# Block products of the gate and up tiles written two at a time, in the matmul order of the plain products

## The chip, the cores and the metric

The kernel runs on one core of a Trainium2 chip. The metric is the device time of one launch in microseconds (us), median of several runs. A core has five engines that each work through a queue of their own in order: PE (TensorE, matrix products), DVE (VectorE), ACT (ScalarE), POOL (GpSimd) and SP (SyncE, which here only issues DMAs). PE loads a 128 x 128 weight tile and then streams columns of a moving operand through it; results accumulate in PSUM, whose banks DVE and ACT read. Everything else lies in SBUF.

## The reference

One step of a hybrid streaming encoder layer, in fp32, on 512 prompt frames and 64 frames of a running stream (576 columns together, the same weights for both):

```python
def swiglu_ffn(x, w_gate_up, w_down):
    gate, up = jnp.split(x @ w_gate_up, 2, axis=-1)
    return (jax.nn.silu(gate) * up) @ w_down
...
    x = x + 0.5 * swiglu_ffn(rms_norm(x, ffn1_norm), ffn1_w_gate_up, ffn1_w_down)
    h = rms_norm(x, mix_norm)
    p = h @ w_in
...
    x = x + merged @ w_out
    x = x + 0.5 * swiglu_ffn(rms_norm(x, ffn2_norm), ffn2_w_gate_up, ffn2_w_down)
```

The model width is 1024, the FFN's inner width 2816. Between the two FFNs stands the mixer: a projection to seven blocks of 1024, two depthwise convolutions with gates, and three more 1024 x 1024 products. A final RMSNorm follows.

## The kernel before

**Layout.** Features lie on the 128 partitions, frames in the columns, so an activation is a list of 128 x 576 tiles. A moving operand is one half of such a tile: columns 0 to 287 (the first half) or 288 to 575 (the second half); H is 288. The two halves' results go to the two PSUM banks of one tile made by `psum2()`; there are four such tiles.

**Precision.** Each fp32 value is split in a high part (type fp32r) and a low part, the rest. A product takes three matmuls: weight high by activation high, weight high by activation low, weight low by activation high. `SIX` (L56) is the order in which a plain product does its six, for each 128 rows of the contraction: high-high and high-low on the first half, the same on the second, then low-high on the first and on the second half.

**FFN.** The 22 inner tiles of 128 go in four groups (`GROUPS`, L42: 5, 5, 6 and 6 tiles). A group makes its hidden tiles (gate, up, SiLU, product) and then multiplies them by its rows of `w_down` into 8 output tiles; the first two of these are interleaved by `both`. The first `PLAIN` tiles (3 in the first FFN, 1 in the second) use plain products. The rest, 19 and 21, use `pair` (L735): a scheme that replaces the eight half-size block products of gate and up by seven, on sums and differences of weight blocks and activations. Each of the seven block products contracts 512 features (KU = 4 tiles), has 288 columns and so 4 x 3 = 12 matmuls. Which half of a tile each of the seven streams is set by `Forms.operands`:

```python
return first[:KU], t2, t1, t3, first[KU:], second[KU:], t4
```

`first` and `second` are the halves of the normed input, t1 and t3 first halves and t2 and t4 second halves of the summed tiles. So products 1, 5 and 6 (counted from 0) stream second halves and the other four first halves.

**Order of work in a pair.** For each block product n: fetch its weight unit (`ws.get`), take a bank (`bank()`, the two banks of a PSUM tile in turn), issue its 12 matmuls one after another, then issue the DVE and ACT steps of product n-1 (`steps`: copies, sums and differences, and in `gate` the SiLU). What remains of a pair (`up`, `hidden`, `parts`) waits in `rest` and is issued one step after each product of the next pair.

**Weights.** `Stream` holds the weight units in the order of their use. SP loads raw weights (six buffers). `add` forms sums of blocks on DVE. `begin` casts the high part on ACT; for three of the seven units of a pair (products 0, 4 and 6) it also writes the negated high part on ACT and lets a POOL DMA add the raw weights to it, which gives the low part. For the other four a DVE subtraction (`end`) gives it. `get(n)` runs this ahead: casts are issued up to six units past n. High and low parts take slots in turn in two pools of eight buffers, so eight units fit; a cast waits until PE has used the unit that had the slot.

Of the kernel before, what the change touches and what calls it, by code (L numbers as in the profile page):

```python
# [10 lines left out]
AF = mybir.ActivationFunctionType  # L11
ALU = mybir.AluOpType
# [5 lines left out]
FT = DFF // P  # L18
SEQ = 512
DSEQ = 64  # L20
KU = KT // 2
T = SEQ + DSEQ
H = T // 2
# [27 lines left out]
PLAIN = {"f1": 3, "f2": 1}  # L51
# [4 lines left out]
SIX = ((0, 0), (1, 0), (0, 1), (1, 1), (2, 0), (2, 1))  # L56
# [47 lines left out]
def tile_encoder_step(  # L104
# [41 lines left out]
    def ttile(dt=F32):  # L146
        return tmp.tile([P, T], dt, tag="tmp", name=nm("tmp"))

    def psum2():
        return mmps.tile([P, 2, 512], F32, tag="mm", name=nm("mm"))  # L150

    spare = []

    def bank():

        if not spare:
            t = psum2()
            spare.extend((t[:, 0, :], t[:, 1, :]))
        return spare.pop(0)

    def halves(ap):
        return ap.rearrange("p (s n) -> p s n", s=2)
# [1 line left out]
    def half(ap, s):  # L164
        return ap[:, s * H : (s + 1) * H]
# [27 lines left out]
    class Stream:  # L193
# [108 lines left out]
    ws = Stream(6)  # L302
    plan = {}
# [60 lines left out]
    for k in FIRST_KS:  # L364
        for name in FIRST:
            r = ws.raw(ffn1_gu, row, k, gu_col(*name[1:]))
# [49 lines left out]
    behind = []  # L416
# [189 lines left out]
    xg = []  # L606
# [83 lines left out]
    def ffn(f, xg, sums, finish, forms, R=None, todo=()):  # L690
        todo = list(todo)

        rest = []


        def plain(i, hs):
# [35 lines left out]
                for step, p in todo.pop(0):  # L732
                    step(p)

        def pair(i, hs, last):  # L735
            qu, uu, t, cu = (ttile() for _ in range(4))
            q1, u2, u3, u4 = half(qu, 0), half(qu, 1), half(uu, 0), half(uu, 1)
            q = []

            def q7():  # L740
                dve.tensor_tensor(u3, q[3], u2, op=ALU.add)
                dve.tensor_tensor(half(cu, 1), u3, q[2], op=ALU.subtract)

            def gate():
                dve.tensor_tensor(half(t, 1), q[5], u4, op=ALU.add)
                dve.tensor_tensor(t, t, R, op=ALU.mult)
                sca.activation(t, t, AF.Silu)

            steps = (
                lambda: sca.copy(q1, q[0]),  # L750
                lambda: dve.tensor_tensor(u2, q[1], q1, op=ALU.subtract),
                lambda: dve.tensor_tensor(u4, q[2], u2, op=ALU.subtract),
                q7,
                lambda: dve.tensor_tensor(half(t, 0), q[4], q1, op=ALU.add),
                gate,
            )
            for n, xs in enumerate(bs):
                w = ws.get(plan[f, "s", i][n])
                q.append(bank()[:, :H])
                for k in range(KU):  # L760
                    (whi, wlo), (xh, xl) = w, xs[k]
                    for m, (l, r) in enumerate(((whi, xh), (whi, xl), (wlo, xh))):
                        pe.matmul(
                            q[n], l[:, k, :], r, start=k == m == 0, stop=k == KU - 1 and m == 2
                        )
                if n > 0:
                    steps[n - 1]()
                if rest:
                    rest.pop(0)()

            hs.append(None)
            at = len(hs) - 1

            def up():
                if last:
                    dve.tensor_tensor(t, t, R, op=ALU.mult)
                dve.tensor_tensor(half(cu, 0), q[6], u3, op=ALU.add)

            def hidden():
                dve.tensor_tensor(cu, cu, t, op=ALU.mult)  # L780
                hs[at] = high(cu)

            def parts():
                hs[at] = hs[at], low(cu, hs[at])

            rest.extend((up, hidden, parts))

        for g, grp in enumerate(GROUPS):
            hs = []
            for i in grp:  # L790
                if i < PLAIN[f]:
                    plain(i, hs)
                    continue
                if i == PLAIN[f]:
                    bs = forms.operands(xg)
                pair(i, hs, grp[-1] == FT - 1)
            while rest:
                rest.pop(0)()
            spare.clear()
            if grp[-1] < FT - 1:  # L800
                for j, ps in enumerate(both([(f, "d", g, j) for j in range(2)], hs)):
                    update(j, ps, R)
                for j in range(2, KT):
                    update(j, product((f, "d", g, j), hs), R)
            else:
                finish(g, hs)
# [390 lines left out]
```

## Time and profile before

| What | Value |
|---|---|
| median of three runs | 1302.98 us (1302.82 to 1303.01) |
| the profiled execution's own time | 1303.07 us |
| its span, first to last instruction | 1301.3 us |
| granted TensorE clock, mean | 0.998 |
| DMA, mean over the span | 168 GB/s |

Engines' busy times count a matmul from its start to its modelled end; matmuls overlap, so a busy PE does not tell at what pace they follow each other. That is read from starts on the timeline, where one row merges neighbouring instructions of one group: the start in us, the time from the start of the first to the end of the last, engine, line, operation, tiles (written<-read, buffer numbers left out), shape, and how many. The names of weight tiles are `u`, `g` and `act`, by the pool that the unit lies in; they change from unit to unit, so that a row of matmuls ends where the unit changes. The line is always L80, that of a helper which keeps the program's order. In brackets stands the engine's idle time before the row and what ended it.

### The profile page before, as it was taken

Reading aid. Unit: us, or ns where it says so; the run is one execution under the profiler, and the core shown is the slowest. Engines: PE = TensorE matmul, PEld = TensorE weight load, DVE = VectorE, ACT = ScalarE, POOL = GpSimd, SP = SyncE. Lnnn points to the kernel's source line nnn. Section 1 sums busy time; section 2 is a strip of 40 time slices with the busy share of each in tenths; the row PEclk is TensorE's granted clock in tenths of the full one; section 3 lists DMA queues with packets and bytes.
Section 4 is the critical chain, followed back from the end, with each engine's and each line's share of the span. In section 5 each row is a group of like instructions: output and inputs, shape, how many; then the busy total and the mean of one; then the engine's idle time right before and its main releaser. Section 6 shows DMA issues by size and latency. Waiting matters only on the chain.

```text
span 1301.3 us, 25714 instructions
## 1 busy us (share of the span) xinstructions
PE 1286.3 (99%) x9746; PEld 1282.5 (99%) x9746; DVE 892.0 (69%) x1460; ACT 778.5 (60%) x1374; POOL 400.5 (31%) x502
## 2 busy tenths in 40 slices
PE   9999999999999999999999999999999999999997
PEld 8999999999999999999999999999999999999996
DVE  6758758748945899888895260336967848847955
ACT  8755655645677655555554684457665655654664
POOL 4242332332242544322221322222142141241233
PEclk9999999999999999999999999999999999999999
DMA  9797787886798797877775978776687796796784
GB/s 245 141 189 160 148 185 157 165 192 147 152 195 182 167 216 173 175 166 170 172 168 125 199 158 178 154 166 142 138 169 165 162 192 149 163 206 136 161 178 107
DMA packets 290108, 218.40 MB, mean 168 GB/s; under 512 B 15680, under 2 KB 251200, under 8 KB 289984
## 3 DMA queue, kind: packets, MB, share of 16 engines
q0 software_dynamic: 60768, 100.30, 46.4%
q1 hardware_dynamic: 227488, 115.62, 31.4%
q8 instruction: 77, 1.26, 0.4%
q10 hardware_dynamic: 1728, 0.84, 0.2%
q14 instruction: 47, 0.39, 0.1%
HBM read 113.81 MB, written 2.62 MB: 89 GB/s over the span
## 4 chain that ended last, share of the span: by engine, by line
PE 90%; issue 4%; DMA 2%; ACT 1%; POOL 1%; DVE 1%; DVEq 0%; POOLq 0%; ACTq 0%; SPq 0%
PE mm L80 90%; DMA g<-raw 1%; DMA raw<-in_ffn_w_gate_up_dram 1%; POOL act L80 1%; DVE tmp L80 0%; ACT u L80 0%; DMA gains<-in_params_dram 0%; POOL g L80 0%; ACT tmp L80 0%; ACT g L80 0%; DVE acc L80 0%; ACT act L80 0%; DVE x L80 0%; DVE g L80 0%; POOL tmp L80 0%
## 5 line engine op out<-in xcount | busy, mean ns | idle before, releaser
L80 PE MATMUL mm<-act,u 128*128 128x288 f32 x4686 | 660.9, 294 | 0.7 <-DVE u L80 0.5
L80 PEld LDWEIGHTS mm<-act,u 128*128 128x128 f32 x4686 | 630.9, 188 | 1.2 <-DVE u L80 0.7
L80 PE MATMUL mm<-act,g 128*128 128x288 f32 x2766 | 398.6, 294 | 2.1 <-DMA g<-raw 2.0
L80 PEld LDWEIGHTS mm<-act,g 128*128 128x128 f32 x2766 | 376.5, 188 | 2.9 <-DMA g<-raw 2.8
L80 POOL DMA_DIRECT2D u<-raw x204 | 176.3, 864 | 550.4 <-ACT u L80 492.2
L80 PE MATMUL mm<-act,act 128*128 128x288 f32 (+2 forms) x2244 | 307.6, 293 | 1.4 <-DVE act L80 1.4
L80 PEld LDWEIGHTS mm<-act,act 128*128 128x128 f32 x2244 | 297.8, 188 | 2.4 <-DVE act L80 2.1
L80 POOL DMA_DIRECT2D g<-raw x124 | 108.6, 876 | 247.2 <-ACT g L80 188.2
L80 ACT CAST u<-raw 128x512 fp32r<-128x512 f32 (+2 forms) x204 | 117.1, 574 | 108.6 <-PE mm L80 76.5
L80 DVE SCALAR_TENSOR_TENSOR w<-g,prm,w 128x606 f32<-128x606 f32 x232 | 179.3, 844 | 1.4 <-ACT w L80 1.4
L80 DVE TENSOR_TENSOR tmp<-mm,tmp 128x288 f32<-128x288 f32 (+1 forms) x244 | 109.7, 458 | 72.9 <-PE mm L80 53.5
L80 ACT ACTIVATE u<-u 128x512 fp32r<-128x512 f32 (+2 forms) x204 | 121.1, 594 | 6.5
L80 POOL DMA_DIRECT2D act<-raw x90 | 78.9, 876 | 50.6 <-ACT act L80 49.5
L80 DVE SCALAR_TENSOR_TENSOR tmp<-mm,r 128x576 f32<-128x576 f32 x48 | 36.3, 757 | 78.0 <-PE mm L80 77.8
L80 ACT CAST g<-raw 128x512 fp32r<-128x512 f32 (+2 forms) x124 | 67.7, 546 | 35.3 <-DMA raw<-in_ffn_w_down_dram 14.7
L80 ACT CAST act<-tmp 128x576 fp32r<-128x576 f32 x84 | 56.2, 674 | 52.4 <-DVE tmp L80 51.6
L80 ACT CAST g<-w 128x512 fp32r<-128x512 f32 x80 | 49.6, 619 | 63.0 <-DVE w L80 56.6
L80 ACT CAST u<-w 128x512 fp32r<-128x512 f32 x80 | 49.5, 619 | 61.9 <-DVE w L80 55.7
L80 DVE TENSOR_TENSOR act<-tmp,act 128x576 fp32r<-128x576 f32 x80 | 59.3, 754 | 21.3 <-ACT act L80 19.8
L80 ACT ACTIVATE g<-g 128x512 fp32r<-128x512 f32 (+2 forms) x124 | 70.4, 568 | 3.9
L80 ACT CAST act<-raw 128x512 fp32r<-128x512 f32 (+2 forms) x99 | 57.6, 583 | 16.1 <-PE mm L80 11.0
L80 DVE TENSOR_TENSOR w<-raw,raw 128x512 f32<-128x512 f32 x80 | 54.8, 685 | 11.0 <-DMA raw<-in_ffn_w_gate_up_dram 11.0
(88 smaller groups left out, 814.1 us busy)
## 6 DMA issues: line engine op xcount, KB each, us to landing
raw<-in_ffn_w_gate_up_dram SPq DMA_DIRECT2D x173, 256.0 KB, 3.4
u<-raw POOLq DMA_DIRECT2D x145, 256.0 KB, 4.0
raw<-in_w_in_dram SPq DMA_DIRECT2D x112, 256.0 KB, 3.4
act<-raw POOLq DMA_DIRECT2D x80, 256.0 KB, 4.8
raw<-in_ffn_w_down_dram SPq DMA_DIRECT2D x96, 192.0 KB, 3.5
g<-raw POOLq DMA_DIRECT2D x65, 256.0 KB, 3.8
g<-raw POOLq DMA_DIRECT2D x43, 192.0 KB, 4.5
u<-raw POOLq DMA_DIRECT2D x43, 192.0 KB, 4.5
```

The source lines that it names most:

```text
L80: return self.tc.keep_in_program_order(fn(*args, **kwargs))
```

## The change

The seven block products of all pairs of a group are put in one list, `jobs`, and written two at a time. A PSUM tile's two banks hold the two products of a two, and the matmuls of both go in the order of `SIX`, with "product" in the place of "half": per 128 rows of the contraction, high-high and high-low of the one, the same of the other, then low-high of each. Seven is odd, so twos run on over the border of pairs: 0 with 1, 2 with 3, 4 with 5, 6 with 0 of the next pair, 1 with 2, 3 with 4, 5 with 6. In the groups with an odd number of products the last one goes alone. Both weight units are fetched before the first matmul of a two. The steps behind a product (`behind`) are issued after the next two's matmuls, those of both products of the two together; each is followed by one step out of `rest`. `bank` and `spare` are gone. The steps themselves are the same.

```diff
-            for n, xs in enumerate(bs):
-                w = ws.get(plan[f, "s", i][n])
-                q.append(bank()[:, :H])
...
+        def pairs(ps):
+
+            jobs = [(p, n) for p in ps for n in range(7)]
+            before = []
+            for c in range(0, len(jobs), 2):
+                two = jobs[c : c + 2]
+                out = psum2()
+                ops = []
+                for s, (p, n) in enumerate(two):
+                    p.q.append(out[:, s, :H])
+                    ops.append((ws.get(plan[f, "s", p.i][n]), bs[n]))
                 for k in range(KU):
-                    (whi, wlo), (xh, xl) = w, xs[k]
-                    for m, (l, r) in enumerate(((whi, xh), (whi, xl), (wlo, xh))):
-                        pe.matmul(
-                            q[n], l[:, k, :], r, start=k == m == 0, stop=k == KU - 1 and m == 2
-                        )
-                if n > 0:
-                    steps[n - 1]()
-                if rest:
-                    rest.pop(0)()
...
+                    for m, s in SIX:
+                        if s < len(two):
+                            (whi, wlo), (xh, xl) = ops[s][0], ops[s][1][k]
+                            l, r = ((whi, xh), (whi, xl), (wlo, xh))[m]
+                            pe.matmul(
+                                out[:, s, :H], l[:, k, :], r,
+                                start=k == m == 0, stop=k == KU - 1 and m == 2,
+                            )
+                for p, n in before:
+                    p.behind(n)
+                    if rest:
+                        rest.pop(0)()
+                before = two
+            for p, n in before:
+                p.behind(n)
```

On PE, at the start of the first FFN's first pair, before: the first rows of product 0. A row is: line, operation, PSUM tile written, moving operand (`act`, high and low part in turn), weights (`g_96` and `g_97` are the high and low part of unit 0, `u_98` and `u_99` of unit 1), shape.

```order
L80 MATMUL mm_157_742<-act_3_110,g_96_464 128x288
L80 MATMUL mm_157_742<-act_4_111,g_96_464 128x288
L80 MATMUL mm_157_742<-act_3_110,g_97_465 128x288
L80 MATMUL mm_157_742<-act_14_134,g_96_464 128x288
L80 MATMUL mm_157_742<-act_15_135,g_96_464 128x288
L80 MATMUL mm_157_742<-act_14_134,g_97_465 128x288
```

The same place on PE, of the change:

```order
L80 MATMUL mm_147_724<-act_3_110,g_96_464 128x288
L80 MATMUL mm_147_724<-act_4_111,g_96_464 128x288
L80 MATMUL mm_147_724<-act_77_278,u_98_493 128x288
L80 MATMUL mm_147_724<-act_102_524,u_98_493 128x288
L80 MATMUL mm_147_724<-act_3_110,g_97_465 128x288
L80 MATMUL mm_147_724<-act_77_278,u_99_494 128x288
```

Unit 1's high part has moved from the 13th to the 3rd matmul and its low part from the 15th to the 6th; unit 0's low part from the 3rd to the 5th.

On ACT, in the second group of the first FFN, at the end of a pair, before. The ACTIVATE on `tmp` is the pair's SiLU; a CAST into `u` or `g` makes a high part, the ACTIVATE after it the negated copy; the CAST of `act` makes the high part of a hidden tile; the COPY from `mm` is step 0 of the next pair.

```order
L80 CAST g_364_1851<-w_361_1831 128x512
L80 ACTIVATE tmp_337_1718<-tmp_337_1718 128x576
L80 CAST u_372_1877<-raw_313_1579 128x512
L80 ACTIVATE u_373_1878<-u_372_1877 128x512
L80 CAST g_378_1903<-raw_355_1793 128x512
L80 ACTIVATE g_379_1904<-g_378_1903 128x512
L80 COPY tmp_367_1870<-mm_366_1854 128x288
L80 CAST act_381_1923<-tmp_338_1719 128x576
```

The same place on ACT, of the change:

```order
L80 CAST g_365_1851<-w_361_1816 128x512
L80 CAST u_368_1857<-raw_309_1559 128x512
L80 ACTIVATE u_369_1858<-u_368_1857 128x512
L80 ACTIVATE tmp_355_1804<-tmp_355_1804 128x576
L80 CAST g_375_1899<-raw_350_1773 128x512
L80 ACTIVATE g_376_1900<-g_375_1899 128x512
L80 CAST u_377_1904<-w_374_1897 128x512
L80 CAST act_379_1933<-tmp_356_1805 128x576
```

The cast and the negation of one unit stood behind the SiLU and now stand ahead of it, two units being fetched at once; the copy of step 0 has moved behind the hidden tile's cast.

More of the change, by code (lines that the diff above doesn't have):

```diff
@@ L150, in psum2 @@
         return mmps.tile([P, 2, 512], F32, tag="mm", name=nm("mm"))
[L152 to L159, printed above, removed]
     def halves(ap):
@@ L691, in ffn @@
         todo = list(todo)
-        rest = []
+        rest, bs = [], None
         def plain(i, hs):
@@ L733, in forming @@
                     step(p)
[L735 to L755, printed above, removed]
-            )
-            for n, xs in enumerate(bs):
-                w = ws.get(plan[f, "s", i][n])
-                q.append(bank()[:, :H])
-                for k in range(KU):
-                    (whi, wlo), (xh, xl) = w, xs[k]
-                    for m, (l, r) in enumerate(((whi, xh), (whi, xl), (wlo, xh))):
-                        pe.matmul(
-                            q[n], l[:, k, :], r, start=k == m == 0, stop=k == KU - 1 and m == 2
-                        )
-                if n > 0:
-                    steps[n - 1]()
-                if rest:
-                    rest.pop(0)()
[L771 to L786, printed above, removed]
@@ L792, in ffn @@
                     plain(i, hs)
[L793 to L796, printed above, removed]
+            if bs is None:
+                bs = forms.operands(xg)
+            pairs([Pair(i, hs, grp[-1] == FT - 1) for i in grp if i >= PLAIN[f]])
             while rest:
                 rest.pop(0)()
-            spare.clear()
             if grp[-1] < FT - 1:
```

36 lines of the change are left out of this document (added).

## The prediction

> **What bounds the kernel now.** I read the page's engine shares first.
>
> ```profile
> span 1301.3 us, 25714 instructions
> ...
> PE 1286.3 (99%) x9746; PEld 1282.5 (99%) x9746; DVE 892.0 (69%) x1460; ACT 778.5 (60%) x1374; POOL 400.5 (31%) x502
> ```
>
> PE is busy for 99% of the span. DVE and ACT have a third of their time free. So what counts is the time from one matmul to the next, and then PE's waits. The view of PE's waits, whole run:
>
> ```profile
> PE mm L80 <- DMA g<-raw: 2.0, 2, 1.5
> PE mm L80 <- DVE act L80: 1.7, 3, 0.8
> PE mm L80 <- POOL eps L80: 1.0, 1, 1.0
> PE mm L80 <- DVE acc L80: 0.5, 1, 0.5
> PE mm L80 <- DVE u L80: 0.5, 1, 0.5
> ```
>
> 8 waits, 5.7 us in all: there is almost no wait to remove, only pace to gain. So I compare the pace of the two orders on the timeline of PE, which merges rows of one group (start, length, count). First the block products, one weight unit a row, in a stretch of the first FFN without waits; seven starts make a pair:
>
> ```profile
> 131.19 1.74 PE L80 MATMUL mm<-act,g 128*128 128x288 f32 x12
> 132.77 1.74 PE L80 MATMUL mm<-act,u 128*128 128x288 f32 x12
> 134.35 1.74 PE L80 MATMUL mm<-act,g 128*128 128x288 f32 x12
> 135.93 1.76 PE L80 MATMUL mm<-act,u 128*128 128x288 f32 x12
> 137.53 1.76 PE L80 MATMUL mm<-act,g 128*128 128x288 f32 x12
> 139.13 1.74 PE L80 MATMUL mm<-act,u 128*128 128x288 f32 x12
> 140.71 1.76 PE L80 MATMUL mm<-act,g 128*128 128x288 f32 x12
> 142.31 1.74 PE L80 MATMUL mm<-act,u 128*128 128x288 f32 x12
> ```
>
> The steps are 1.58 us four times and 1.60 us three times, 11.12 us for 84 matmuls: 132.4 ns each. The rows start at product 2 of a pair. The three slow ones, at 135.93, 137.53 and 140.71, are products 5, 6 and 1, and these are just the ones whose moving operand is the second half of a 576-column tile (`operands`, L178). So a product costs 131.7 ns a matmul on first halves and 133.3 on second halves. Now the plain order, in a down product of the same FFN (18 a row, starts 2.37 us apart) and in the mixer (24 a row, 3.12 us apart):
>
> ```profile
> 269.18 2.54 PE L80 MATMUL mm<-act,u 128*128 128x288 f32 x18
> 271.55 2.53 PE L80 MATMUL mm<-act,g 128*128 128x288 f32 x18
> ```
>
> ```profile
> 502.71 3.28 PE L80 MATMUL mm<-act,u 128*128 128x288 f32 x24
> 505.83 3.28 PE L80 MATMUL mm<-act,act 128*128 128x288 f32 x24
> ```
>
> That is 2.37/18 = 131.7 ns and 3.12/24 = 130.0 ns, with first and second halves mixed in equal parts. The same six-matmul order thus has two paces.
>
> **The change part by part.** *Pace.* There are 19 + 21 = 40 pairs, 40 x 84 = 3360 matmuls, 40 x 11.12 = 444.8 us. No matmul, weight load, DVE, ACT or POOL instruction is added or removed; only order changes. At 131.7 a pair takes 84 x 2.37/18 = 11.06 us: **-0.06 x 40 = -2.4 us**. At 130.0 it takes 10.92 us: -0.20 x 40 = -8.0 us. The bound on the other side: if alternating products do nothing, 0; if every product ran at the second halves' 1.60 us, 7 x 1.60 = 11.20, +3.2 us. I take -2.4: the down products stand in the same FFN, just behind the block products, and run at 131.7 each time. Two of the seven twos (2 with 3) have first halves only, and one (5 with 6 of the second pair) second halves only; these are not patterns that a plain product has. Were they to stay as they are, the gain would be 0.02 us (3.18 against 24 x 2.37/18 = 3.16) in each of 80 mixed twos, -1.6 us.
>
> The Trainium skill ("TensorE: Matmul & The Clock Gate", Back-to-back issue gap) gives the warm gap as N/2.4 + 2.5 ns, by the columns alone; for 288 columns an estimate from it is 122.5 ns, in any order. By that rule the order would be worth nothing; the rows above, with 130.0 to 133.3 at one N, speak against it.
>
> *Waits at the start of each FFN.* A product of two needs the low half of its second weight unit at the 6th of 24 matmuls, 0.66 us after the two start. Before, it was needed at 1.58 + 0.26 = 1.84 us. So that need comes 1.2 us earlier, and behind it, on PE's queue, stand the other 19 matmuls of both products. Where the units are just in time, this shows. In the first FFN, PE's timeline, then POOL's row for product 7, with the median landing from the page's list of DMAs:
>
> ```profile
> 54.85 1.88 PE L80 MATMUL mm<-act,g 128*128 128x288 f32 x12
> ...
> 57.47 1.59 PE L80 MATMUL mm<-act,u 128*128 128x288 f32 x10 [0.48 <-DVE u L80]
> 58.90 0.42 PE L80 MATMUL mm<-act,g 128*128 128x288 f32 x2
> 60.84 1.60 PE L80 MATMUL mm<-act,g 128*128 128x288 f32 x10 [1.51 <-DMA g<-raw]
> ...
> 63.86 1.76 PE L80 MATMUL mm<-act,g 128*128 128x288 f32 x12
> ```
>
> ```profile
> 58.67 0.86 POOL L80 DMA_DIRECT2D u<-raw  x1 [0.32 <-ACT tmp L80]
> ```
>
> ```profile
> u<-raw POOLq DMA_DIRECT2D x145, 256.0 KB, 4.0
> ```
>
> Products 4 and 5 start at 54.85. The low half of 5 is there at 57.47, so the two stop after five matmuls and end at 57.47 + 19 x 0.132 = 59.98, 1.1 us after 58.90. Products 6 and 7 reach the low half of 6 at about 60.8 without much of a wait, but 7's lands at 58.67 + 4.0 = 62.7 and 19 matmuls remain: 65.2 against 63.86, +1.3. The other of the two waits for a `g` DMA (2.0 in all, 1.5 of it here, so 0.5), which comes later in this part, then finds PE late and goes: **+0.8**. In the second FFN, products 6, 7, 12, 13 and 14 on PE's timeline:
>
> ```profile
> 926.07 1.76 PE L80 MATMUL mm<-act,u 128*128 128x288 f32 x12
> 927.67 1.74 PE L80 MATMUL mm<-act,g 128*128 128x288 f32 x12
> ...
> 935.59 1.76 PE L80 MATMUL mm<-act,u 128*128 128x288 f32 x12
> 937.19 2.17 PE L80 MATMUL mm<-act,g 128*128 128x288 f32 x12
> 939.21 1.74 PE L80 MATMUL mm<-act,u 128*128 128x288 f32 x12
> ```
>
> 7's low half was read at 927.67 + 0.26 = 927.9 without a wait, and would now be wanted at 926.07 + 0.66 = 926.7: 0 to 1.2 us of wait, by how early it was there. Product 13, which lost 0.4 us before (939.21 - 937.19 is 2.02 where 1.59 is usual), would be wanted 1.2 us earlier too, and PE comes later by the first wait. I take **+0.9** for both. Together +1.7; between 0 (if ACT's new order brings the requests forward as much as they are needed earlier) and +4.
>
> *In the steady stretch.* Two units are fetched at once, so ACT's casts wait for the release of both slots at the end of a two, and SiLU stands behind them, no longer ahead. Before, at the end of a pair (ACT, POOL, PE):
>
> ```profile
> 1114.45 0.69 ACT L80 ACTIVATE tmp<-tmp 128x576 f32<-128x576 f32 x1 [0.85 <-DVE tmp L80]
> 1115.04 0.61 ACT L80 CAST u<-raw 128x512 fp32r<-128x512 f32 x1
> ```
>
> ```profile
> 1116.61 0.86 POOL L80 DMA_DIRECT2D u<-raw  x1 [3.70 <-DVE w L80]
> ```
>
> ```profile
> 1123.13 1.76 PE L80 MATMUL mm<-act,u 128*128 128x288 f32 x12
> ```
>
> The request at 1116.61 lands near 1120.6 by the median of 4.0; the low half is first read at 1123.13 + 0.26 = 1123.4: 2.8 us spare. The cast stood behind the SiLU and began 3.0 us after the product 5 ahead of it ended (a pair before this row: 1123.13 - 11.12 = 1112.0). Now a cast that is second of its two begins one cast and one negation (about 0.6 us each, by the row of the cast) after the two's end and is wanted three twos and 0.66 us after that end, 3 x 3.16 + 0.66 = 10.1 us. Cast, negation, wait for POOL and landing take 1120.6 - 1115.04 = 5.6: 10.1 - 1.2 - 5.6 = 3.3 us spare. So I cost the steady stretch at nothing. Evacuation moves one product later and four PSUM tiles still hold eight products; the next FFN part gets its last hidden tile at its fifth or sixth group of 12 matmuls, later than the gate chain that now follows the last product (SiLU's 0.69 in the row above, and the few DVE operations around it, of which the page has one of 576 columns):
>
> ```profile
> L80 DVE TENSOR_TENSOR act<-tmp,act 128x576 fp32r<-128x576 f32 x80 | 59.3, 754 | 21.3 <-ACT act L80 19.8
> ```
>
> Four such and the SiLU are 3.7 us, where four groups of 12 take 6.3. Without that cover each group end would pay the difference.
>
> **Sum.** 1303.07 (the profiled execution; 1301.3 of span and 1.8 around it; the median shown is 1302.98) - 2.4 + 1.7 = **1302.4 us**.
>
> **Rivals.** *The mixer's pace* (0.28). The plain order can run at 130.0, and does so for 24 a row over most of the mixer. If the twos fall into that pace: 1303.07 - 8.0 + 1.7 = 1296.8. If the down products behind them keep it, some 1930 matmuls x 1.7 ns more: 1293.6. For it: one order, two paces, so the pace is not fixed by the order. Against it: no product in either FFN of this trace has it. *Only halves count, or nothing* (0.18). Then the gain is 1.6 or 0: 1303.2 to 1304.8. For it: first-half products in one bank already run at the down products' 131.7. The rule of the Trainium skill named above would end here, at 1304.8. *Late second unit* (0.14, slower). Twos with a DMA-made low half in second place are 7, 11 and 13 of each fourteen, some 57 in all. If ACT reaches the cast over 3.3 us later than I put it, PE stops after five matmuls each time; at 0.2 us each on half of them, 28 x 0.2 = +5.6 on top of the sum: 1308.0. At 0.1 us it would just undo the gain of pace. For it: the cast above did begin 3.0 us late; against: SiLU no longer stands ahead of it. The forecast itself has 0.40.
>
> **How the numbers follow.** 0.2% is 2.6 us, about what a measurement of this kernel can tell from no change: 1300.4 to 1305.6. Faster: the mixer's pace, 0.28, and a part of the forecast where some twos have it, 0.08: 0.36. Slower: the late unit, 0.13, and 0.02 of the third case with starts at +4. Same: 0.49. The range leaves out the slow rival above 1306 and the lower end of the fast one below 1294: 1294.0 to 1306.0. The likeliest case's own range is 1300.0 to 1304.7.
>
> **What would show it.** Starts of rows of 24 in the FFN's PE timeline: 3.16 us apart is my step, 3.12 the mixer's pace, 3.18 or more no gain. Down products at 2.37 or 2.34 us. PE's waits: more than 5.7 us, with the new ones at 55 to 63 and 926 to 938. If waits stand beyond 80 us in the first FFN, the late unit is right and I am wrong. If first-half twos step otherwise than mixed ones, halves count and not order.

## The result and the profile after

The changed kernel takes 1313.42 us (median of six runs, 1307.89 to 1314.94) where the kernel before takes 1302.93 beside it (six runs, 1302.18 to 1304.06): a ratio of 1.007, 95% interval 1.0058 to 1.0082. It is slower, by 10.5 us; that is less than 1%, but clear of the noise. The forecast was 1302.4, and the range ended at 1306.

The profiled execution took 1313.85 us. The page's line of engine shares:

```profile
PE 1291.7 (98%) x9746; PEld 1286.9 (98%) x9746; DVE 894.1 (68%) x1460; ACT 779.7 (59%) x1374; POOL 400.8 (31%) x502
```

PE, DVE, ACT and POOL have the same number of instructions as before and DVE, ACT and POOL nearly the same busy time. The view of PE's waits, the rows that differ from those of before:

```profile
PE mm L80 <- DMA g<-raw: 3.1, 2, 1.9
...
PE mm L80 <- DVE tmp L80: 1.7, 1, 1.7
PE mm L80 <- DVE u L80: 1.4, 1, 1.4
PE mm L80 <- DMA u<-raw: 1.4, 2, 1.2
```

With the three rows that stayed (1.8 where it was 1.7, 1.0 and 0.5) that is 10.9 us of waits where there were 5.7. So waits explain about half of the 10.8 us between the two profiled executions. For the rest I set the starts of the 9746 matmuls of both traces beside each other, stretch by stretch (each figure is the time from the first start of a stretch to the first start of the next one, after minus before):

| Stretch (us in the trace of before) | Matmuls | Change, us |
|---|---|---|
| up to the first pair | 316 | +0.19 |
| first FFN, first group: pairs, then down products (48 to 106) | 168 + 240 | +1.23 - 0.76 |
| the five groups of pairs in which nothing waits | 2352 | -0.74 |
| first FFN, last group of pairs (298 to 364) | 504 | +1.25 |
| its down products and the mixer's first product | 336 | -0.05 |
| the rest of the mixer and the second FFN's plain products (409 to 917) | 3904 | **+5.68** |
| second FFN, first group of pairs (917 to 961) | 336 | +1.45 |
| second FFN, last down products (1252 to 1266) | 108 | +2.48 |
| all other stretches | | +0.05 |

The largest term lies in a part of the program that the change doesn't touch. PE's timeline in the mixer, where before showed starts 3.12 us apart:

```profile
502.34 3.32 PE L80 MATMUL mm<-act,act 128*128 128x288 f32 x24
505.50 3.32 PE L80 MATMUL mm<-act,u 128*128 128x288 f32 x24
```

Now they are 3.16 us apart: 131.7 ns a matmul and not 130.0, without a wait, at the same granted clock (0.998 in both). The last down products of the first FFN, just ahead of the mixer, have changed pace too. PE's timeline, before and then after:

```profile
397.52 2.53 PE L80 MATMUL mm<-act,u 128*128 128x288 f32 x18
399.89 2.53 PE L80 MATMUL mm<-act,g 128*128 128x288 f32 x18
```

```profile
375.85 2.50 PE L80 MATMUL mm<-act,u 128*128 128x288 f32 x18
378.19 2.50 PE L80 MATMUL mm<-act,g 128*128 128x288 f32 x18
```

The starts were 2.37 us apart and are now 2.34, 130.0 ns a matmul. The two paces have changed places, and the border is the first sum over partitions in the mixer (`rstd`, four matmuls with ones). The mixer has two more such sums, at 696 and 722 us in the trace of before: between them its matmuls ran at 131.7 and outside at 130.0, and in the change it is the other way round. Where did the down products get 130.0 from? PE's timeline at the waits in the last groups:

```profile
360.16 0.40 PE L80 MATMUL mm<-act,g 128*128 128x288 f32 x1 [1.15 <-DMA g<-raw]
...
367.67 3.65 PE L80 MATMUL mm<-act,u 128*128 128x288 f32 x26 [0.22 <-DMA u<-raw]
...
1263.31 3.76 PE L80 MATMUL mm<-act,g 128*128 128x288 f32 x26 [1.95 <-DMA g<-raw]
```

The wait of 0.2 us ahead of 367.67 is the last thing before the new pace: the rows behind it run at 130.0. All three rows stand in the last group of an FFN, and all wait for the low half of a weight unit. That low half needs a cast and a negation on ACT, then a request on POOL. ACT's timeline ahead of the first of them:

```profile
347.40 0.69 ACT L80 ACTIVATE tmp<-tmp 128x576 f32<-128x576 f32 x1 [1.33 <-DVE tmp L80]
350.07 0.68 ACT L80 CAST act<-tmp 128x576 fp32r<-128x576 f32 x1 [1.99 <-DVE tmp L80]
...
353.21 0.62 ACT L80 CAST g<-raw 128x512 fp32r<-128x512 f32 x1
353.86 0.64 ACT L80 ACTIVATE g<-g 128x512 fp32r<-128x512 f32 x1
```

and POOL's request:

```profile
356.75 1.75 POOL L80 DMA_DIRECT2D g<-raw  x2 [9.53 <-ACT g L80]
```

The first row is a pair's SiLU, the second the cast of its hidden tile. Between them DVE does three operations: the second multiplication by R (0.76 us), `up` (0.45) and the product (0.76), 1.97 us in all, and ACT stands still for 1.99. In the old order a product of PE lay between `up` and `hidden`, so ACT had weight casts to do there, and then waited for 0.19 us only; ACT's timeline of before, the same SiLU and hidden tile's cast:

```profile
343.58 0.69 ACT L80 ACTIVATE tmp<-tmp 128x576 f32<-128x576 f32 x1 [1.51 <-DVE tmp L80]
...
347.09 0.68 ACT L80 CAST act<-tmp 128x576 fp32r<-128x576 f32 x1 [0.19 <-DVE tmp L80]
```

Now `hidden` is issued directly behind `up`, and the weight casts behind it stand waiting for up to 2 us. The second multiplication by R is there in the last group of each FFN alone.

So my theory was: **(1)** hidden casts that block ACT make the late waits; **(2)** the order of six has two stable paces, and a wait or four odd matmuls can switch between them; so 0.2 us of wait cost 5.7 us of mixer. The rivals: the order in twos itself gives the mixer its pace, or the late low halves come from POOL's and SP's order.

### The profile page after: what moved, and what is told of

The parts are those of the page before. It is cut to its first block, busy times and chain, and to the rows that moved or that the text cites. A ratio compares the mean times of both kernels' runs of the same rounds, so it can differ in the third digit from the quotient of the medians.

```text
span 1312.1 us, 25698 instructions
## 1 busy us (share of the span) xinstructions
PE 1291.7 (98%) x9746; PEld 1286.9 (98%) x9746; DVE 894.1 (68%) x1460; ACT 779.7 (59%) x1374; POOL 400.8 (31%) x502
## 4 chain that ended last, share of the span: by engine, by line
PE 73%; issue 14%; DMA 5%; DVE 3%; POOL 3%; ACT 1%; POOLq 0%; SPq 0%; DVEq 0%; ACTq 0%
PE mm L80 73%; DMA raw<-in_ffn_w_gate_up_dram 2%; DMA u<-raw 2%; POOL g L80 1%; DVE tmp L80 1%; POOL u L80 1%; DMA g<-raw 1%; DVE w L80 1%; POOL act L80 1%; DVE g L80 1%; ACT u L80 0%; DVE act L80 0%; ACT tmp L80 0%; DMA raw<-in_ffn_w_down_dram 0%; DVE u L80 0%
## 5 line engine op out<-in xcount | busy, mean ns | idle before, releaser
L80 PE MATMUL mm<-act,u 128*128 128x288 f32 x4686 | 805.0, 294 | 5.0 <-DVE tmp L80 1.7
L80 PEld LDWEIGHTS mm<-act,u 128*128 128x128 f32 x4686 | 687.4, 188 | 6.3 <-issue 1.9
L80 PE MATMUL mm<-act,g 128*128 128x288 f32 x2766 | 538.8, 294 | 3.1 <-DMA g<-raw 3.1
L80 PEld LDWEIGHTS mm<-act,g 128*128 128x128 f32 x2766 | 430.3, 188 | 3.8 <-DMA g<-raw 3.8
L80 ACT ACTIVATE tmp<-tmp 128x576 f32<-128x576 f32 x47 | 32.2, 684 | 58.0 <-DVE tmp L80 58.0
```

Of the source, the lines that this page charges most:

```text
L80: return self.tc.keep_in_program_order(fn(*args, **kwargs))
```

## Experiments

### e1: hidden one two later

```diff
+                left = len(rest)
                 for p, n in before:
                     p.behind(n)
-                    if rest:
+                    if left:
+                        left -= 1
                         rest.pop(0)()
```

> The changed kernel with one edit: of what waits in `rest`, only what stood there before the two is issued behind it, so a pair's `hidden` and the high cast of its tile on ACT are issued one two (3.2 us) later. Theory A (ACT's queue): in the last group of each FFN the cast of the hidden tile waited 1.99 us on ACT for the longer chain with the extra multiplication by R, and the casts behind it came late. Then the PE waits near 358 (1.3 us), 367 (0.4) and 1263 us (1.95 us) are gone, about -3.3 us, and with no wait at 367 the mixer keeps 3.12 us a row of 24: another -5.6 us; in all 1304 to 1305.5 us, in every round. Theory B (the order in twos itself sets the mixer's pace): the waits go, the mixer stays at 3.16 us a row, 1309 to 1311 us. Theory C (the late low halves come from POOL's and SP's order, not ACT's): the waits stay, 1312 to 1315 us.

Measured: 1304.33 us, ten runs from 1304.01 to 1305.63, against 1303.16 of before; ratio 1.001 (1.000 to 1.0019). All three late waits are gone, and the mixer has its old pace; PE's timeline of e1:

```profile
503.03 3.28 PE L80 MATMUL mm<-act,u 128*128 128x288 f32 x24
506.15 3.28 PE L80 MATMUL mm<-act,act 128*128 128x288 f32 x24
```

ACT's timeline, the same place:

```profile
346.52 0.69 ACT L80 ACTIVATE tmp<-tmp 128x576 f32<-128x576 f32 x1 [1.33 <-DVE tmp L80]
...
350.26 0.67 ACT L80 CAST act<-tmp 128x576 fp32r<-128x576 f32 x1 [1.73 <-DVE tmp L80]
...
351.36 0.62 ACT L80 CAST g<-raw 128x512 fp32r<-128x512 f32 x1
```

ACT still waits for DVE, but with two casts and a copy done first: the cast of `g` from raw weights comes 351.36 - 346.52 = 4.84 us behind the SiLU, where it came 353.21 - 347.40 = 5.81 behind. That 1.0 us is enough here: no wait is left. One line of order is worth 9 us: Theory A; the order in twos is not what sets the mixer's pace.

### e6: without the second multiplication by R

In the last group of each FFN the hidden tiles lack the factor R, and nothing else differs from the change.

```diff
-                    if self.last:
-                        dve.tensor_tensor(t, t, R, op=ALU.mult)
```

> The changed kernel without the second multiplication by R of the last group of each FFN (12 DVE instructions of 0.76 us left out, so those hidden tiles lack the factor). Theory A (the hidden cast on ACT waits for the chain SiLU, R, up, product): the chain is 0.76 us shorter, ACT's 1.99 us ahead of the cast of the hidden tile at 350 and 1245 us falls to about 1.2 us, as in the groups before, which have no such multiplication and no wait; the PE waits near 358, 367 and 1263 us fall below 0.5 us in all, the mixer runs at 3.12 us a row of 24: 1304 to 1305.5 us. Theory B (the last group is late for another reason, its smaller units of 384 rows behind the pairs): the waits stay within 0.5 us of 1.3, 0.4 and 1.95 us, 1309 to 1314 us.

Measured: 1304.07 us, one run. No wait in either last group, the mixer at 130.0 ns. ACT's timeline:

```profile
345.13 0.69 ACT L80 ACTIVATE tmp<-tmp 128x576 f32<-128x576 f32 x1 [0.90 <-DVE tmp L80]
346.64 0.67 ACT L80 CAST act<-tmp 128x576 fp32r<-128x576 f32 x1 [0.82 <-DVE tmp L80]
```

1.99 us became 0.82, more than the 0.76 that the multiplication takes. The late waits come from this chain; the other six groups, which have no such multiplication, have no such waits.

### e2: two more sums in the mixer, kernel before

The two sums' results are not used.

```diff
         xs = xg if raw else xn
+        if j == 2:
+            ss.total()
...
     for j in range(KT):
+        if j == 1:
+            ss.total()
         for b, of in ((1, c_of), (2, cv_of), (0, b_of)):
```

> The kernel before with two more sums over partitions in the mixer (four matmuls with ones each, their result unused): one ahead of the fifth product, one ahead of the fourth product of the next part, 15 products (720 matmuls) between them. Theory A (the plain order has two stable paces and four odd matmuls flip it): rows of 24 are 3.12 us apart ahead of the first sum, 3.16 us between the two and 3.12 us behind the second; the time is 8 x 0.13 = 1.0 us for the matmuls and 720 x 1.67 ns = 1.2 us for the pace, in all 1305.1 us. Theory B (pace set by data, buffers or weights): 3.12 us throughout, 1304.0 us.

Measured: 1305.16 us (1304.71 to 1305.74), against 1303.16; ratio 1.0015 (1.0006 to 1.0025). PE's timeline around both sums:

```profile
424.54 3.29 PE L80 MATMUL mm<-act,act 128*128 128x288 f32 x24
427.66 0.69 PE L80 MATMUL mm<-tmp,ones_r 128*128 128x288 f32 x4
428.19 3.32 PE L80 MATMUL mm<-act,u 128*128 128x288 f32 x24
431.35 3.32 PE L80 MATMUL mm<-act,act 128*128 128x288 f32 x24
...
523.00 0.69 PE L80 MATMUL mm<-tmp,ones_r 128*128 128x288 f32 x4
523.52 3.28 PE L80 MATMUL mm<-act,u 128*128 128x288 f32 x24
526.64 3.28 PE L80 MATMUL mm<-act,act 128*128 128x288 f32 x24
```

3.12 us ahead of the first sum, 3.16 behind it, 3.12 again behind the second, with the same weights and data (each sum takes a PSUM tile, so the products behind it lie one tile further on; but all four tiles take turns within each pace). The pace is a state of PE's stream, and four matmuls switch it, in both directions. Theory A, to 0.1 us.

### e4: one more sum in the mixer, changed kernel

Only the first of the two edits of e2, on the change.

> The changed kernel with one more sum over partitions (four matmuls with ones, result unused) ahead of the fifth product of the mixer. Theory A (two stable paces, flipped by four odd matmuls): where the profiled execution of the change had 3.16 us a row of 24 in the mixer, rows behind the new sum are 3.12 us apart up to the sum near 690 us, 3.16 for the 192 matmuls up to the next and 3.12 again behind that: 1313.4 - 5.6 + 0.5 to 1 = about 1308.5 us; rounds in which the mixer was fast anyway become slow, so the spread of about 5 us stays and only its halves change places. Theory B (the mixer's pace comes from buffers or weights): 1314 us, rows at 3.16 us throughout.

Measured: 1311.88 us (four runs, 1309.28 to 1314.07), so the spread stayed, as Theory A has it. The profiled execution is the other of the two cases:

```profile
367.58 3.70 PE L80 MATMUL mm<-act,u 128*128 128x288 f32 x26 [0.22 <-DMA u<-raw]
...
429.87 0.69 PE L80 MATMUL mm<-tmp,ones_r 128*128 128x288 f32 x4
430.40 3.32 PE L80 MATMUL mm<-act,u 128*128 128x288 f32 x24
433.56 3.32 PE L80 MATMUL mm<-act,act 128*128 128x288 f32 x24
```

Up to 429.87 the program is the changed kernel, word for word. Its wait at 367 has the same 0.22 us, but the 26 matmuls behind it take 3.70 us and not 3.65: the gaps between the starts of the two matmuls on both sides are 0.516 us in the change and 0.513 here. This time the wait left the stream at 131.7, `rstd` brought the mixer to 130.0, and the added sum turned that to 131.7. So two waits that the trace can hardly tell apart were followed by two different paces; what decides is not shown. It would explain the changed kernel's spread of 7 us (its runs lie at 1307.9 to 1309.7 and at 1313.3 to 1314.9), and why e1, which has no late wait, is spread over 1.6 us only; but no profile was taken of a run of the change near 1308.

### e3: two at a time, matmuls in the old order

```diff
-                for k in range(KU):
-                    for m, s in SIX:
-                        if s < len(two):
+                for s in range(len(two)):
+                    for k in range(KU):
+                        for m in range(3):
```

> The changed kernel with the matmuls of a two in the old order (12 of the one product, then 12 of the other); fetching, slots and steps stay two at a time. Theory A: the late group's waits come from ACT's order, which is unchanged, but the second unit's low half is needed 1.2 us later: the wait of 1.3 us near 358 shrinks to about 0, the waits at the FFN starts shrink by about 2 us, the one near 1263 (in the down products) stays at about 1.9; pace of the pairs back to 132.4 ns a matmul (+1.0 us). If a wait remains near 367 the mixer is at 3.16 us a row, else at 3.12: 1306.5 us with 3.12, 1312 us with 3.16. Theory B (twos' matmul order is what costs the time): 1303 us, no wait above 0.5 us beyond those of before.

Measured: 1306.21 us (ten runs, 1305.40 to 1311.95), ratio 1.0033 (1.0021 to 1.0044). PE's timeline of the profiled execution (1305.4 us):

```profile
365.56 3.70 PE L80 MATMUL mm<-act,u 128*128 128x288 f32 x26 [0.55 <-DMA u<-raw]
...
1255.18 3.69 PE L80 MATMUL mm<-act,g 128*128 128x288 f32 x26 [0.53 <-DMA g<-raw]
```

The wait in the pairs of the last group is gone. Of the two in the down products one is 0.55 us where it was 0.22, the other 0.53 where it was 1.95 (I had expected 1.9). So issuing two at a time brings late waits with the old order of matmuls too, 1.1 us in all; with the new order they are 3.3. The mixer was at 130.0 here, though a wait stood ahead of it; two of the ten runs lie at 1311.4 and 1312.0, some 5.6 us above the others, as a mixer at 131.7 would give (not profiled).

### e8 and e9: the openings of the FFNs

In e8 (on e1) the steps of the second FFN's plain product are issued behind the first two:

```diff
+                for _ in range(0 if before else 2):
+                    if rest:
+                        rest.pop(0)()
                 left = len(rest)
```

> The kernel of e1 with one edit: what waits in `rest` from the second FFN's plain product (its gate and hidden steps) is issued behind the matmuls of the first two, not of the second. Theory A (the 1.9 us wait near 930 us is for the PSUM tile that the plain product's gate multiplication on DVE releases at 931.86, not for weights): the multiplication runs right behind R, near 927.9 us, the wait is gone, the stage from 915.6 to 960.5 us takes 1.4 to 1.9 us less: 1302.6 us. Theory B (my prediction's: the second unit's low half is late there): the wait stays or comes back on a weight tile, 1304.0 to 1304.5 us.

Measured: 1303.60 us (1302.82 to 1304.36), before 1303.35; ratio 1.0004 (0.9994 to 1.0014). In the changed kernel PE waited here for DVE; the two timelines:

```profile
931.10 0.75 DVE L80 TENSOR_TENSOR tmp<-mm,r 128x576 f32<-128x576 f32 x1
```

```profile
931.99 0.50 PE L80 MATMUL mm<-act,u 128*128 128x288 f32 x2 [1.74 <-DVE tmp L80]
```

In e8 the multiplication `tmp<-mm,r`, which reads the PSUM tile that the third two needs, is done ten us sooner:

```profile
921.80 0.75 DVE L80 TENSOR_TENSOR tmp<-mm,r 128x576 f32<-128x576 f32 x1
```

```profile
939.76 0.40 PE L80 MATMUL mm<-act,u 128*128 128x288 f32 x1 [0.39 <-DMA u<-raw]
```

The 1.74 us are gone, so that wait was for the PSUM tile. The wait at 939.76 is a new one and takes back part. It is for the low half of product 14, the first of its two, and not for one of the two that I had forecast here (7 and 13). In this execution, the fastest of the ten, the group is 0.23 us longer than before (in the change it was 1.45). In e9, whose second FFN is the same, it is 1.20 us longer, and PE's timeline has

```profile
940.16 0.40 PE L80 MATMUL mm<-act,u 128*128 128x288 f32 x1 [1.46 <-DMA u<-raw]
```

POOL's request for that low half stands at 935.58 us in e8 and at 934.92 in e9, 4.2 and 5.2 us ahead of these rows. So this wait differs from one execution to the next, and the median of e8 lies 1.0 us above the 1302.6 of Theory A.

e9 adds the old order of matmuls for the pairs of the first FFN's first group (its list of matmuls is sorted by product).

> The kernel of e8 with the two pairs of the first FFN's first group in the old order of matmuls (12 and 12), still two fetched at a time. Theory A (there PE waits for low halves because a two needs the second unit's 1.2 us sooner, while ACT and DVE are just in time): the first group costs 0.5 to 1.4 us less than in e8, as it did where all pairs had that order: 1301.3 to 1302.1 us if e8 gives 1302.6. Theory B (the fetch of two at a time costs it there): no change against e8.

Measured: 1303.22 us (1302.54 to 1305.13), ratio 1.000 (0.9991 to 1.001). The first FFN's first group with its down products takes 0.10 us less than before and in e8 0.43 more: a difference of 0.53, where at least 0.5 was expected. In the median it is 0.4, less than the 0.5 to 1.4 that was forecast, and within the noise. e9 is not free of the change's costs: its six groups of pairs that have twos and no wait are 0.90 us shorter than before, and the opening of the second FFN, with the wait above, takes 1.20 back. So in the whole kernel the order in twos is worth nothing that can be measured.

### e5: other orders of six

In six groups, output tiles 2 and 5 begin with another order; no matmul is added to e1.

```diff
+                    update(j, product((f, "d", g, j), hs, six=OTHER[f, g] if j in (2, 5) else None), R)
```

> The kernel of e1 with, in six of the eight groups of down products (the last group of each FFN is left alone), another order of the first six matmuls of output tiles 2 and 5. The order of halves is 0 0 1 1 0 1 everywhere else; here it is, by group: 000111, 010101, 110010, 001110, 001011, 011001. No matmul is added. Theory A (two stable paces of one order; a foreign order of a few matmuls can flip them without any cost): behind at least one of the six, the down products run at 130.0 ns a matmul (18 in 2.34 us) where they ran at 131.7 (2.37 us), and where tile 2 flips them tile 5 flips them back; 3 products of 30 matmuls each make 0.15 us a group, so the whole time stays 1304.0 to 1304.5 us. Theory B (only matmuls of other stationary operands or waits flip): 131.7 ns throughout, 1304.4 us.

Measured: 1305.12 us, one run. Theory A failed in its second part: none of the six orders brought 130.0. One, 001110 in the second FFN's first group, brought a third pace, which lasted to the end of the group:

```profile
987.36 2.58 PE L89 MATMUL mm<-act,u 128*128 128x288 f32 x18
...
991.39 2.58 PE L89 MATMUL mm<-act,u 128*128 128x288 f32 x18
```

30 matmuls in 4.03 us: 134.4 ns.

### e10 and e12: halves that alternate

On e9, the halves of the second summed tile change places in `combine` and `operands`, so that a pair's products stream F S F S F S F; the product on the first half goes first.

```diff
-                (half(d, 0), half(b1, 1), half(b2, 1), ALU.subtract),
-                (half(d, 1), half(b2, 0), half(c, 1), ALU.subtract),
+                (half(d, 1), half(b1, 1), half(b2, 1), ALU.subtract),
+                (half(d, 0), half(b2, 0), half(c, 1), ALU.subtract),
...
-            return first[:KU], t2, t1, t3, first[KU:], second[KU:], t4
+            return first[:KU], t2, t1, t4, first[KU:], second[KU:], t3
```

> The kernel of e9 with two edits: the second FFN's first group has the matmuls of its pairs in the old order of 12 and 12 too; and the two halves of the second summed tile change places (product 3 then streams a second half and product 6 a first half), with the product on the first half ahead in each two. The halves of a pair's products then alternate, F S F S F S F: of the seven twos of two pairs six mix a first and a second half and one, 6 with 0 of the next pair, has first halves only. Theory A (the pace of a two is set by which halves it streams): every mixed two takes 131.7 ns a matmul, the 133.65 of (5,6) and the 132.5 of (4,5) go, groups of 420 and 504 matmuls run at 131.7 instead of 132.07, about -0.16 and -0.2 us a group, -1.1 us in all; the second FFN's first group comes back to within 0.3 us of its length before. In all 1301 to 1302 us. Theory B (the pace hangs on the products' places in the two or on their weights): 132.0 to 132.1 ns stay, 1302.2 to 1303.2 us.

Measured: 1307.72 us (1307.34 to 1308.07), ratio 1.0035 (1.0022 to 1.0049): a miss of 6 us, and the most telling one. From 77 us to a wait of 0.1 us at 258 us pairs and down products alike ran at 130.0, but for the twos on first halves only, at 131.6 (0.90, 0.41 and 1.08 us less than before in three stretches); from there on the pairs ran at 131.7, as expected (0.36 us less in each group of 504). But behind a wait of 0.06 us at 362 us the down products fell to 134.4, and the mixer then ran at 131.7, which costs the 5.7 us. Nor did the second FFN's first group come back to within 0.3 us: product 14's low half made PE wait for 1.71 us there, and the group was 1.57 us longer than before. PE's timeline in the second and in the last group's down products:

```profile
167.85 2.50 PE L80 MATMUL mm<-act,u 128*128 128x288 f32 x18
170.19 1.72 PE L80 MATMUL mm<-act,g 128*128 128x288 f32 x12
...
371.10 2.58 PE L80 MATMUL mm<-act,u 128*128 128x288 f32 x18
373.52 2.58 PE L80 MATMUL mm<-act,g 128*128 128x288 f32 x18
```

18 in 2.34 us, then 18 in 2.42. So a stream that mixes halves hands on whatever pace it has. The pairs of before end with products on one half only, and that may be what brings the stream to the same pace each time. It fits the profiles: where the pairs end so and no wait comes behind them, the mixer was at 130.0 each time, and in the three kernels with alternating halves it was at 131.7. No run tests it by itself.

e12 drops the rule that the first half goes ahead.

> The kernel of e10 without its rule that the product on the first half goes ahead: in (1,2), (3,4) and (5,6) of every second pair the second half goes ahead. Theory A (which halves a two mixes decides, not which is ahead): the same pace as e10, 131.7 ns a matmul, within 0.1 us a group. Theory B (a change of the order of halves costs at each border, as the 133.7 ns of the twelve matmuls behind a first-half two suggests): one or two more twelves of 133 to 134 ns a pair, +0.05 to +0.1 us for each two pairs, up to 1 us in all.

Measured: 1308.48 us, one run; the groups without waits are 0.28 to 0.34 us shorter than before, where those of e10 at that pace are 0.29 to 0.36: which half is ahead doesn't matter. Its mixer was at 131.7 too.

### e11 and e13: switching on purpose

Four matmuls with ones ahead of the second group's pairs, on e10.

```diff
+            if g == 1:
+                kick = psum2()
+                for s in range(2):
+                    for v in range(2):
+                        pe.matmul(kick[:, s, :H], ones_r, half(xg[0][v], s), start=v == 0, stop=v == 1)
```

> The kernel of e10 with four matmuls with ones (halves 0 0 1 1, result unused, 0.53 us) ahead of the pairs of the second group of each FFN. Theory A (they flip the pace of any stream that mixes halves as a plain product does, until another wait or kick): the pairs, the down products behind them or both run at 130.0 ns a matmul from about 105 and 992 us on, down to the next first-half two at least; if the pace holds over the groups, 2.9 to 4 us less than e10 in the first FFN and a mixer whose pace is turned round (+5.6 us). Theory B (only a stream that is as even as the mixer's keeps 130.0): the pairs and down products stay at 131.7, the mixer at 130.0, 1.1 us more than e10.

Measured: 1306.24 us, one run. In the first FFN they switched 131.7 to 130.0, which held for 230 us over three groups, up to a wait of 0.24 us at 338; in the second FFN they did nothing; and the mixer was at 131.7. Comparing the starts around all such fours of the traces shows what differs: the stream at 131.7 repeats after 12 matmuls and the program's order after six, so it can stand in two ways, and in one of them the four left it at 131.7. So it stood at `rstd` in e11 and e12: their last down products ran at 131.7, as in the kernel before, but with the pattern standing the other way, and the mixer stayed at 131.7 without a wait in between. e13 therefore moves the four by one product of 30 matmuls, in the second FFN alone, with the first FFN as in e9.

> The first FFN as in e9, the second as in e10 (alternating halves), and the four matmuls with ones of e11 in the second FFN alone, ahead of the last down product of its first group and not behind it. In e11 the slow pattern, which takes 12 matmuls, stood at the end of that group at 132 131 131 131 134 131 ns from the product's start, and there the four did not flip it; one product of 30 matmuls sooner it stands six matmuls shifted, at 131 133 128 133 132 133, the place at which they flipped it in all other cases. Theory A (the pace hangs on the phase between the order of six and the pattern of twelve): that product, the pairs and the down products of the second to the fourth group run at 130.0 ns until a wait, the mixer stays at 130.0 (its pace was set in the first FFN, as in e9): about -0.5 us in the first FFN, +1.6 in the second's first group, +0.5 for the four, -3.6 behind them: 1301.3 us. Theory B (no such phase; what four matmuls do is chance): 131.7 ns there, 1303.9 us.

Measured: 1303.73 us (eleven runs, 1300.23 to 1304.68), ratio 0.9998 (0.9989 to 1.0007). The pace came as expected; PE's timeline:

```profile
988.30 2.53 PE L80 MATMUL mm<-act,u 128*128 128x288 f32 x18
990.67 1.75 PE L80 MATMUL mm<-act,g 128*128 128x288 f32 x12
992.25 0.69 PE L80 MATMUL mm<-act,ones_r 128*128 128x288 f32 x4
992.78 2.50 PE L80 MATMUL mm<-act,u 128*128 128x288 f32 x18
995.12 1.72 PE L80 MATMUL mm<-act,g 128*128 128x288 f32 x12
```

2.37 us for 18 ahead of the four and 2.34 behind, and so on to the last down products, where a wait of 0.4 us at 1253 ended it: 3.94 us gained from the pairs of the second group on. The time did not follow; it is near Theory B's. The opening of the second FFN lost 3.21 us and not the 1.6 that I had put in (the last section shows how), the last down products with their wait lost 0.46, a wait behind them 0.52, and the first FFN gained nothing. No version here beats the kernel before.

## Why the prediction was wrong

*What bounds the kernel* was right: only pace and waits moved. The steps:

- **Pace, -2.4: mis-sized; -1.0 was measured.** The five groups without waits gain 0.74 us in 2352 matmuls, 0.31 ns each, for all 3360 -1.06 us. I had taken the plain FFN pace of 131.7 for every two. Most mixed twos have it, but the two on second halves only (5 with 6) still runs at 133.65, and the first 12 matmuls behind a two on first halves only at 133.7 and more. (Twos on first halves only are 2 with 3 and, in the second pair, 3 with 4; `operands` stands at L593, not L178.) The rival "only halves count" named this (-1.6); e10 and e12, which alternate the halves, get the forecast 131.7.
- **Waits at the start of the first FFN, +0.8: right.** +0.47 us with the down products (+0.67 with what lies ahead); the wait for a low half that the twos need sooner and the loss of the later `g` wait came as worked out, and e9 takes them away.
- **Waits at the start of the second FFN, +0.9: the size nearly (+1.45), the mechanism not.** PE waited 1.74 us for a PSUM tile. `gate` of the plain product waits in `rest` and is now issued behind the second two, and the third two needs its tile (e8). I had followed weights only, and not asked when each PSUM tile comes free. The waits forecast for products 7 and 13 came in no run; with the tile free, it is product 14's low half that PE waits for, 0.39 us in e8 and 1.46 to 1.84 in e9 to e13.
- **The steady stretch at nothing: the step that failed.** The 3.3 us spare were reckoned from casts that stand ahead of the SiLU. I wrote that "SiLU no longer stands ahead of it" but not that the hidden tile's cast now does, with 2 us of DVE work in front of it in the last groups. The five groups in between had no wait; the last ones paid +1.25 us (first FFN, in the pairs) and +2.48 (second FFN, in the down products). e1 and e6, which take the hidden tile's cast out of the way or shorten its chain, take both away. The rival "late second unit" had the mechanism, ACT behind in its queue, but spread it over 57 units and priced it at 5.6 us.
- **The mixer: put at nothing, with no step for it, and the largest miss.** I had the rows ("one order, two paces, so the pace is not fixed by the order") and used them for a gain in the FFNs only. The same rows say that the mixer's 130.0 could be lost. It was: +5.68 us. e1, e2 and e4 show how: a wait of 0.2 us turned the pace ahead of `rstd`, and `rstd` turned it again. Why the stream has several paces stays open.
- *The cover at the group ends* held: no hidden tile came late for its down products.

With the failed step mended (e1: 1304.33) the sum is 1303.07 - 1.0 + 0.5 + 1.45 = 1304.0, so the measured terms add up. The Trainium skill ("TensorE: Matmul & The Clock Gate", Back-to-back issue gap) gives the formula that the prediction used for isolated matmuls, and for a stream of weight loads and matmuls one sustained figure for a number of columns, about 81 ns at 128 and 131 ns at 512. With 288 columns these runs show 130.0, 131.7, 133.65 and 134.4 ns at one granted clock (1.00), so the traces don't agree here that one figure goes with a number of columns.

## What to carry to other kernels

When two steps of a chain are issued closer together, list what stands behind the second on its engine: a consumer that waits holds up what stands behind it in its queue (here weight casts, behind 1.99 us on ACT), and the price shows far away, at a DMA. When a trace shows one instruction sequence at two paces, treat the faster one as something the change can lose, and look for what resets it (here perhaps streams on one half only) before replacing that. A repeatable time may rest on such a reset; a spread of several us after a change may mean that a wait now decides it.

## What the runs showed of the hardware

PE's pace at 288 columns is a state. The same six-matmul order has paces of 130.0, 131.7 and 134.4 ns; it kept the first two for hundreds of us and the third for 40 (e10), and a wait (0.06 us in e10) or four matmuls of another kind (e2) can change it. Which one follows a wait differed between executions (the change and e4). Why is open; the traces show it on matmul starts only.

In one execution a wait of 1.83 us was followed by half of PE's clock. e13, PE's timeline and then a stretch of 2 us (length, PE's busy time and matmuls, granted clock, DMA share, GB/s):

```profile
940.98 2.21 PE L80 MATMUL mm<-act,u 128*128 128x288 f32 x10 [1.83 <-DMA u<-raw]
942.98 2.71 PE L80 MATMUL mm<-act,g 128*128 128x288 f32 x12
```

```profile
942.90:944.90 2.00, 2.00 (x11) 0.50 0.98 208
```

The gap between the two matmuls' starts was 2.13 us. Behind it came one at 237 ns and three at the usual pace, then 15 at 171 to 240 ns (13 of them 240), where the granted clock was 0.50: 1.55 us lost over the wait itself. In the other traces a gap of up to 2.05 us, and in the change one of 2.24 (ahead of 1263.31), was followed by one slow matmul only, so its length alone doesn't decide it. The Trainium skill ("TensorE: Matmul & The Clock Gate", Part 1: The HAM clock gate) names an idle window of about 3.4 us for that; here the clock fell once behind 1.83 us of idle, and in the change, behind 1.95, it did not.
